# One pool of eight PSUM banks in place of four fixed shares, in a two-layer transformer block on one core

## The chip, the core and the metric

The kernel runs on one core of a Trainium2 chip. The metric is the device time of one execution in microseconds (us). The program is written with a tile framework: the code names tiles, pools and operations, and a scheduler orders each engine's instructions when the program is built. The chip then runs five fixed streams, one for each engine, that wait for each other by semaphores.

## What is computed

Two layers of a diffusion-transformer block work on 256 tokens x and 256 context tokens ctx of width 1024. Each layer projects both, runs three branches (a neighbourhood attention, a gated MLP and a multi-head latent attention with rank-compressed keys), merges them under sigmoid gates, and applies a squared-ReLU MLP:

```python
h = modulate(rms_norm(x, g_norm1[i]), sh1, sc1)
p = h @ w_in[i]
y_na = merge_heads(neighbourhood_attention(q_na, k_na, v_na, k_na_c, v_na_c, na_rpb[i]))
y_gm = spatial_gating(gelu(u), gelu(v), gm_ln_g[i], gm_ln_b[i], gm_w_s[i], gm_b_s[i])
y_mla = merge_heads(dense_attention(q_mla, concat(k_mla_c, k_mla), concat(v_mla_c, v_mla)))
mix = (g0 * (y_na @ na_w_o) + g1 * (y_gm @ gm_w_o) + g2 * (y_mla @ mla_w_o)) @ w_out
x_new = x + gt1 * mix
x_new = x_new + gt2 * squared_relu_mlp(modulate(rms_norm(x_new, g_norm2[i]), sh2, sc2), w1, w2)
```

In layer 0 the context tokens take the same way, as a second stream that attends to itself alone. In layer 1 they only give keys and values.

## The kernel before

Activations lie transposed (features on partitions, 512 tokens on the free axis: 256 of x, 256 of ctx). Large products run as three fp32r matmuls (`mm3`, lines 287 to 289): weights are split in a high and a low part by ScalarE (`wh`, line 115) and VectorE (`wl`, line 116). Each weight block of 512 KB is loaded by SyncE into one of three `raw` buffers.

A layer runs through these stages: projections (`gemm_b`, tiles `b_ps`), the `u` blocks of the gated MLP, neighbourhood attention (NA), the merge of the gated-MLP branch (`merge`: eight pairs of a `gate` and a `z` block), key, value and query products of the latent attention (MLA; tiles `kv`, `qm`, transposes `h_tr`), MLA attention, the merges of the two other branches, the output product and norm, then the MLP (`f1_chunk`, tiles named `f`, and `out_chunk`, tiles `o_ps`).

Both attentions go through `soft_pv`, once for each of four pairs of heads. For each stream v and each half qt of its queries it runs one step for the pair: two score tiles `S` on TensorE (line 410 and 411 in NA, 417 in MLA); then for each head a bias add on VectorE (line 443, NA and stream x only), the row maximum `nm` (445), the exponential with its row sum on ScalarE (448), the reciprocal (450) and the scaling of `P` on VectorE (451), the transposes of `P` into a tile `pt` on TensorE (454) and the copy of `pt` to `PT` on ScalarE (456). After two steps the products with the values go to a tile `pv` or `pvm` (460). Rows are 512 keys wide for x and 256 for ctx. `P` and `PT` have two buffers each.

`soft_pv` notes each score matmul in `marks`, and the following merge takes them as its pace: `gemm_a` ties each three matmuls of a gate or z block behind one mark on TensorE (`issue_after`), so that they may stand between the score matmuls of the attention and not ahead of them.

Every PSUM tile is one bank (128 x 512 fp32) and comes from `psum(tag, name)` at lines 47 and 48. The tag is `mm` for gemm tiles, `s` for score tiles, small transposes and sums, `pt` for the transposes of `P` and two modulation sums, `pv` for attention outputs and the broadcast norm. Tiles of one tag share its banks: 4, 2, 1 and 1. The scheduler takes instructions by priority, which is the order of the code (a block under `high_priority` counts as 400 places earlier), as soon as their inputs and their tiles' buffers are there.

The norm at the end of a stage (`norm_stream`, lines 237 to 247) adds squares over chunks (`sumsq`: ScalarE line 255, VectorE line 256), sums over partitions on TensorE (`st_ps`), takes a power on GpSimd (line 241), builds a diagonal on VectorE (244) and broadcasts it on TensorE (`rstd_b`, line 247).

Of the kernel before, what the change touches and what calls it, by code (L numbers as in the profile page):

```python
# [7 lines left out]
F32 = mybir.dt.float32  # L8
# [18 lines left out]
def hybrid_block_kernel(tc, a, out):  # L27
# [3 lines left out]
    mm = nc.tensor.matmul  # L31

    from contextlib import ExitStack, nullcontext
    with ExitStack() as es:
        def pool(name, bufs=1, **kw):
            return es.enter_context(tc.tile_pool(name=name, bufs=bufs, **kw))
# [8 lines left out]
        pp = pool("ps", space=PSUM)  # L45

        def psum(tag, name):
            return pp.tile([128, 512], F32, tag=tag, name=name, bufs={"mm": 4, "s": 2, "pt": 1, "pv": 1}[tag])


        def g2(name, dt=F32R):
# [88 lines left out]
        def mod_finish(ps, w, dsts, modT, bmod, streams):  # L140

            t = tmp2("mod_sb")
            vec.tensor_copy(t[:, :w], ps[:, :w])
            pst = psum("s", "mod_t")
            for i in range(w // 128):
                nc.tensor.transpose(pst[:, i * 128:(i + 1) * 128], t[:, i * 128:(i + 1) * 128], ident)
            for i in range(w // 128):
                v4 = pst[:, i * 128:(i + 1) * 128].rearrange("p (j r) -> p j r", j=4)
                for v in range(streams):
                    o, b = dsts(modT[:, v, :], i), dsts(bmod, i)  # L150
                    i0 = v4[:, :, v]
                    if len(o.shape) == 3:
                        i0 = i0.rearrange("p (a b) -> p a b", a=2)
                    vec.tensor_tensor(out=o, in0=i0, in1=b, op=ALU.add)

        def mod_quarter(l, q, modT, bmod, streams):

            ps = psum("pt", "mod_ps")
            for kb in range(4):
                for kk in range(2):  # L160
                    raw = g2("rawm", F32)
                    nc.sync.dma_start(out=raw, in_=a["wmod1"][l, q, kb][:, kk * 512:kk * 512 + 512])
                    mod_cols(ps, raw, 0, 128, 2 * kb + kk)
                yield
            mod_finish(ps, 128, lambda m, i: m[:, 0:16].rearrange("p (a c) -> p a c", a=2)[:, :, 2 * q:2 * q + 2], modT,
                       bmod, streams)

        def mod_group(l, g, modT, bmod, streams):
            ps = psum("mm", "mod_ps")
            for k in range(KC):  # L170
                raw = load(a["wmod"][l, g - 2, k])
                mod_cols(ps, raw, 0, 256, k)
                yield
            mod_finish(ps, 256, lambda m, i: m[:, 8 * g:8 * g + 8].rearrange("p (j i) -> p j i", i=2)[:, :, i], modT, bmod,
                       streams)
# [371 lines left out]
        for l in range(L):  # L547
# [192 lines left out]
            for j in range(4):  # L740
# [6 lines left out]
                pv = psum("pv", "pv")  # L747
# [94 lines left out]
            for j in range(4):  # L842
                pv = psum("pv", "pvm")
# [226 lines left out]
```

## Time and profile before

| | |
|---|---|
| median of three runs | 1402.77 us (1400.9 to 1403.62) |
| profiled execution, its own time | 1402.83 us |
| its span in the trace | 1400.8 us |
| TensorE busy | 1370.2 us, 98% |
| VectorE busy | 957.4 us, 68% |
| ScalarE busy | 704.7 us, 50% |
| mean granted TensorE clock | 1.00 |

The page gives one profiled execution. Its busy times are unions over an engine's instructions; TensorE's matmuls overlap each other, so the mean duration of one is longer than its distance to the next.

### The profile page before, as it was taken

What the parts mean: (1) busy time and instruction counts of PE and PEld (TensorE: products, weight loads), DVE (VectorE), ACT (ScalarE), POOL (GpSimd) and SP (SyncE); (2) the same over time, 40 slices, a digit from 0 to 9 for tenths busy, and PEclk for the clock granted to TensorE, in tenths of its full rate; (3) what the DMA queues carried; (4) which work ended last, traced back from release to release, by engine and by line L of the source; (5) the groups of instructions that cost most, each with busy time, mean ns of one, the idle gap of its engine ahead of it and who ended that gap; (6) DMA issues with size and microseconds to landing.
All of it is one profiled execution on the core that took longest, in us unless ns stands there. A gap on an engine that the chain in (4) does not pass through costs nothing.

```text
span 1400.8 us, 22572 instructions
## 1 busy us (share of the span) xinstructions
PE 1370.2 (98%) x8438; PEld 1161.8 (83%) x8438; DVE 957.4 (68%) x2071; ACT 704.7 (50%) x1440; POOL 56.9 (4%) x35
## 2 busy tenths in 40 slices
PE   6999999999999999999999999999999999999999
PEld 4788767777676789988888888988888878999998
DVE  4666477665563558899766665786787766877775
ACT  3466256443453346623324233566676665656654
POOL 0110000110000000000000000011002100000000
PEclk9999999999999999999999999999999999999999
DMA  9423542234313465665555552443543434566664
GB/s 331 142 84 106 187 150 90 71 105 123 119 46 114 127 195 168 208 202 172 203 205 188 175 197 89 150 137 94 181 136 99 136 91 136 181 181 180 183 183 148
DMA packets 67214, 210.61 MB, mean 150 GB/s; under 512 B 8609, under 2 KB 9633, under 8 KB 67105
## 3 DMA queue, kind: packets, MB, share of 16 engines
q1 hardware_dynamic: 67104, 209.18, 46.6%
q8 instruction: 66, 1.08, 0.3%
q14 instruction: 44, 0.35, 0.1%
HBM read 208.10 MB, written 1.05 MB: 149 GB/s over the span
## 4 chain that ended last, share of the span: by engine, by line
PE 96%; DVE 1%; DMA 1%; ACT 1%; issue 0%; SPq 0%; POOL 0%; ACTq 0%; DVEq 0%
PE o_ps L287 8%; PE o_ps L289 8%; PE o_ps L288 8%; PE f L288 6%; PE f L287 6%; PE f L289 6%; PE gate L287 5%; PE gate L288 5%; PE gate L289 5%; PE b_ps L287 5%; PE b_ps L288 4%; PE b_ps L289 4%; PE pt L454 3%; PE S L417 2%; PE z L287 2%; PE z L289 2%
## 5 line engine op out<-in xcount | busy, mean ns | idle before, releaser
L115 ACT ACTIVATE wh<-raw 128x512 fp32r<-128x512 f32 (+1 forms) x570 | 353.1, 626 | 515.8 <-PE o_ps L288 179.7
L116 DVE TENSOR_TENSOR wl<-raw,wh 128x512 fp32r<-128x512 f32 (+1 forms) x570 | 385.8, 683 | 178.1 <-ACT wh L115 172.7
L289 PE MATMUL f<-hH,wl 128*128 128x258 f32 (+2 forms) x560 | 180.9, 324 | 0.1
L287 PE MATMUL f<-hH,wh 128*128 128x258 f32 (+2 forms) x560 | 180.4, 323 | 0.5 <-ACT wh L115 0.5
L288 PE MATMUL f<-hL,wh 128*128 128x258 f32 (+2 forms) x560 | 180.4, 324 | 0.2 <-DVE hL L277 0.2
L288 PE MATMUL o_ps<-aL,wh 128*128 128x256 f32 (+1 forms) x544 | 176.1, 327 | 0.0
L287 PE MATMUL o_ps<-aH,wh 128*128 128x256 f32 (+1 forms) x544 | 176.0, 328 | 0.0
L289 PE MATMUL o_ps<-aH,wl 128*128 128x256 f32 (+1 forms) x544 | 175.6, 328 | 0.0
L287 PE MATMUL gate<-hH,wh 128*128 128x512 f32 (+1 forms) x384 | 140.5, 366 | 0.0
L289 PE MATMUL gate<-hH,wl 128*128 128x512 f32 (+1 forms) x384 | 130.3, 339 | 0.0
L288 PE MATMUL gate<-hL,wh 128*128 128x512 f32 (+1 forms) x384 | 130.1, 339 | 0.0
L287 PEld LDWEIGHTS f<-hH,wh 128*128 128x128 f32 x560 | 106.0, 190 | 9.1 <-ACT wh L115 0.7
L289 PEld LDWEIGHTS f<-hH,wl 128*128 128x128 f32 x560 | 106.2, 190 | 8.5 <-DVE wl L116 0.3
L288 PEld LDWEIGHTS f<-hL,wh 128*128 128x128 f32 x560 | 105.9, 190 | 8.5 <-DVE hL L277 0.4
L287 PEld LDWEIGHTS o_ps<-aH,wh 128*128 128x128 f32 x544 | 102.7, 190 | 9.5 <-ACT aH L937 0.8
L288 PEld LDWEIGHTS o_ps<-aL,wh 128*128 128x128 f32 x544 | 103.1, 190 | 8.5
L289 PEld LDWEIGHTS o_ps<-aH,wl 128*128 128x128 f32 x544 | 102.7, 190 | 8.8
L288 PE MATMUL b_ps<-wl,hH 128*128 128x512 f32 (+2 forms) x288 | 108.8, 381 | 0.0
L289 PE MATMUL b_ps<-wh,hL 128*128 128x512 f32 (+2 forms) x288 | 106.3, 381 | 0.0
L287 PE MATMUL b_ps<-wh,hH 128*128 128x512 f32 (+2 forms) x288 | 103.7, 385 | 0.0
L200 DVE SCALAR_TENSOR_TENSOR macc<-rawx,sS,macc 128x512 f32<-128x512 f32 x112 | 78.9, 748 | 32.7 <-DMA rawx<-in_wmod_dram 32.4
L287 PEld LDWEIGHTS gate<-hH,wh 128*128 128x128 f32 x384 | 72.7, 189 | 15.9 <-issue 7.5
(229 smaller groups left out, 2481.3 us busy)
## 6 DMA issues: line engine op xcount, KB each, us to landing
raw<-in_wa_dram SPq DMA_DIRECT2D x147, 512.0 KB, 3.6
raw<-in_w_dram SPq DMA_DIRECT2D x68, 512.0 KB, 3.6
raw<-in_wb_dram SPq DMA_DIRECT2D x32, 512.0 KB, 3.3
raw<-in_wmod_dram SPq DMA_DIRECT2D x32, 512.0 KB, 3.4
rawx<-in_wmod_dram SPq DMA_DIRECT2D x32, 512.0 KB, 4.5
raw<-in_wo_dram SPq DMA_DIRECT2D x24, 512.0 KB, 3.6
rawm<-in_wmod_dram SPq DMA_DIRECT2D x32, 256.0 KB, 6.0
rawx<-in_wmod_dram SPq DMA_DIRECT2D x32, 256.0 KB, 4.2
```

What stands on the lines that cost most here:

```text
L115: act(out=wh[:, :width], in_=src, func=AF.Copy)
L116: vec.tensor_tensor(out=wl[:, :width], in0=src, in1=wh[:, :width], op=ALU.subtract)
L200: summed = vec.scalar_tensor_tensor(out=o, in0=src, scalar=s, in1=o, op0=ALU.mult, op1=ALU.add)
L287: mm(ps, lhsT=sh, rhs=mh, start=first, stop=False)
L288: mm(ps, lhsT=sh, rhs=ml, start=False, stop=False)
L289: mm(ps, lhsT=sl, rhs=mh, start=False, stop=last)
L417: return mm(s, lhsT=Q[h][0:96, q0:q0 + 128], rhs=K[h][0:96, k0:k0 + nk], start=True, stop=True)
L454: nc.tensor.transpose(pt[:, i * 128:(i + 1) * 128], P[:, i * 128:(i + 1) * 128], ident)
```

## The change

```diff
         def psum(tag, name):
-            return pp.tile([128, 512], F32, tag=tag, name=name, bufs={"mm": 4, "s": 2, "pt": 1, "pv": 1}[tag])
+            return pp.tile([128, 512], F32, tag="bank", name=name, bufs=8)
```

All PSUM tiles now carry one tag with eight buffers. The argument `tag` is no longer used. The arithmetic and the number of banks are the same. The scheduler makes another order of it, on all engines.

TensorE in neighbourhood attention of layer 0, x stream, before. `S`, `pt` and `pv` are the attention's tiles, `z` and `yg` belong to the merge of the gated-MLP branch:

```order
L460 MATMUL pv<-PT,vna 64x256 x4
L454 MATMUL pt<-ident,P 128x128 x4
L410 MATMUL S<-naK,naQ 128x512
L411 MATMUL S<-naK,naQL_1070 128x512
L287 MATMUL z<-yg,wh 128x512
L288 MATMUL z<-yg,wh 128x512
L289 MATMUL z<-yg,wl 128x512
L454 MATMUL pt<-ident,P 128x128 x4
L410 MATMUL S<-naK,naQ 128x256
L411 MATMUL S<-naK,naQL_1064 128x256
```

The same place now:

```order
L410 MATMUL S<-naK,naQ 128x512
L411 MATMUL S<-naK,naQL_1064 128x512
L410 MATMUL S<-naK,naQ 128x512
L411 MATMUL S<-naK,naQL_1070 128x512
L460 MATMUL pv<-PT,vna 64x256 x4
L454 MATMUL pt<-ident,P 128x128 x8
L410 MATMUL S<-naK,naQ 128x512
L411 MATMUL S<-naK,naQL_1064 128x512
L410 MATMUL S<-naK,naQ 128x512
L411 MATMUL S<-naK,naQL_1070 128x512
L454 MATMUL pt<-ident,P 128x128 x8
L460 MATMUL pv<-PT,vna 64x256 x8
```

Before, a single score tile, three merge matmuls and four transposes take turns. Now both score tiles of a step stand together, then both heads' transposes; the merge's matmuls have moved behind the last step of the attention. Both attentions of both layers read like this.

TensorE at the norm after the output product of layer 0, before (the x half of the chunks ends some 35 matmuls ahead of `st_ps`):

```order
L289 MATMUL o_ps<-mix,wl 128x256
L287 MATMUL o_ps<-mix,wh 128x256
L288 MATMUL o_ps<-mix,wh 128x256
L237 MATMUL st_ps<-ones,acc_4950 128x1 x2
L289 MATMUL o_ps<-mix,wl 128x256
L287 MATMUL o_ps<-mix,wh 128x256
L288 MATMUL o_ps<-mix,wh 128x256
```

Here `rstd_b` comes another 34 matmuls behind `st_ps`.

The same place now:

```order
L288 MATMUL o_ps<-mix,wh 128x256
L289 MATMUL o_ps<-mix,wl 128x256
L237 MATMUL st_ps<-ones,acc_4950 128x1 x2
L247 MATMUL rstd_b<-diag,ones 128x256
L287 MATMUL o_ps<-mix,wh 128x256
L288 MATMUL o_ps<-mix,wh 128x256
```

Before, 34 matmuls of the ctx half stood between `st_ps` and `rstd_b`, and 35 ahead of `st_ps`. Now `st_ps` follows the last matmul of the x half and `rstd_b` follows `st_ps`. The norms at the end of layer 0 and after the output product of layer 1 have moved in the same way; the two norms of the ctx half in layer 0 still have matmuls ahead of `rstd_b`, but none ahead of `st_ps`.

## Rows read from the trace of the kernel before

**Rows 1.** The page: span, busy time of engines, chain that ended last.

```profile
span 1400.8 us, 22572 instructions
...
PE 1370.2 (98%) x8438; PEld 1161.8 (83%) x8438; DVE 957.4 (68%) x2071; ACT 704.7 (50%) x1440; POOL 56.9 (4%) x35
...
PE 96%; DVE 1%; DMA 1%; ACT 1%; issue 0%; SPq 0%; POOL 0%; ACTq 0%; DVEq 0%
```

**Rows 2.** Stretches (NA, MLA, NA, MLA, MLP): length, busy PE, PEld, DVE, ACT, POOL; clock; DMA.

```profile
183.00:252.00 69.00, 66.82 (x403) 46.97 (x404) 50.43 (x132) 43.57 (x112) 0.00 (x0) 1.00 0.33 107
331.00:435.00 104.00, 104.00 (x551) 72.35 (x550) 58.23 (x138) 50.80 (x125) 0.00 (x0) 1.00 0.30 92
1010.00:1063.00 53.00, 48.52 (x355) 41.32 (x355) 40.06 (x96) 35.08 (x77) 0.00 (x0) 1.00 0.43 127
1107.00:1163.00 56.00, 53.09 (x355) 40.29 (x354) 32.93 (x73) 32.91 (x74) 0.00 (x0) 1.00 0.25 76
1190.00:1225.00 35.00, 35.00 (x292) 34.95 (x292) 28.12 (x62) 22.07 (x45) 0.70 (x1) 1.00 0.61 185
```

**Rows 3.** Timeline, end of MLA in layer 1: start, us, engine, line, [idle before].

```profile
1152.00 1.95 PE L460 MATMUL pvm<-PT,vml 128*64 128x256 f32 x16
...
1157.85 0.68 ACT L448 ACTIVATE P<-S,nm 128x512 f32<-128x512 f32 x1
...
1158.65 0.16 DVE L450 RECIPROCAL r<-sm 128x1 f32<-128x1 f32 x1 [0.91 <-ACT P L448]
...
1158.92 0.49 DVE L451 TENSOR_SCALAR P<-P,r 128x512 f32<-128x512 f32 x1
...
1159.56 0.63 PE L454 MATMUL pt<-ident,P 128*128 128x128 f32 x4 [0.89 <-DVE P L451]
1160.22 0.60 ACT L456 ACTIVATE PT<-pt 128x512 f32<-128x512 f32 x1 [0.93 <-PE pt L454]
...
1160.87 1.95 PE L460 MATMUL pvm<-PT,vml 128*64 128x256 f32 x16 [0.69 <-ACT PT L456]
```

**Rows 4.** Groups by form, VectorE: count, busy us, mean ns, idle before.

```profile
L869 DVE SCALAR_TENSOR_TENSOR xT<-o_ps,modT,xT 128x256 f32<-128x256 f32 x120 | 54.6, 480 | 38.8 <-PE o_ps L289 38.2
L445 DVE TENSOR_REDUCE nm<-S 128x1 f32<-128x512 f32 x64 | 43.8, 686 | 19.4 <-PE S L417 18.8
L256 DVE TENSOR_TENSOR acc<-acc,sq 128x256 f32<-128x256 f32 x49 | 20.2, 420 | 6.1 <-ACT sq L255 5.6
L443 DVE TENSOR_TENSOR S<-S,bias 128x256 f32<-128x256 f32 x32 | 13.6, 428 | 2.7 <-PE S L411 2.6
L445 DVE TENSOR_REDUCE nm<-S 128x1 f32<-128x256 f32 x32 | 13.5, 423 | 20.8 <-PE S L417 13.5 <-PE S L411 7.3
L451 DVE TENSOR_SCALAR P<-P,r 128x256 f32<-128x256 f32 x32 | 11.2, 351 | 0.8
```

**Rows 5.** Groups by form, ScalarE.

```profile
L255 ACT ACTIVATE sq<-xT 128x256 f32<-128x256 f32 x49 | 20.1, 414 | 6.0 <-DMA xT<-in_xT_dram 3.7 <-DVE xT L869 1.0 <-DVE acc L256 0.2
L448 ACT ACTIVATE P<-S,nm 128x256 f32<-128x256 f32 x32 | 15.0, 470 | 0.0
```

**Rows 6.** Chain of waits: start, length, instruction; NA and MLA of layer 1.

```profile
1015.87 0.50 PE S L410
...
1018.04 0.23 PE S L410
1018.27 0.23 PE S L411
...
1111.03 0.86 PE S L417 x2
```

**Rows 7.** Timeline of TensorE at the first norm.

```profile
12.50 1.01 PE L237 MATMUL st_ps<-ones,acc 128*128 128x1 f32 x4
...
15.84 1.22 PE L247 MATMUL rstd_b<-diag,ones 128*128 128x256 f32 x2
```

**Rows 8.** DMA issues: tile, queue, count, KB each, us to landing.

```profile
bias<-in_nab_dram SPq DMA_DIRECT2D x16, 256.0 KB, 3.2
```

## The prediction

> **What bounds the kernel now.** I read the page first: TensorE is busy for 1370.2 of 1400.8 us, and the chain that ended last is TensorE for 96% [rows 1]. Only some 30 us of the span are TensorE's idle time, so nothing that makes another engine faster can bring more than that, while any order that leaves TensorE without work costs its full length. Next I read the busy time of the four attention stretches [rows 2]. There the softmax runs on VectorE and ScalarE, a chain of dependent instructions, and yet TensorE is busy for 66.8 of 69, 104 of 104, 48.5 of 53 and 53.1 of 56 us: its idle time in all four is 2.2 + 0 + 4.5 + 2.9 = 9.6 us. The reader is to see that the merge's gate and z matmuls fill the waits of the softmax. The third view is the end of the MLA attention of layer 1 [rows 3], one place where the fill has run out before the attention has. There TensorE waits 0.89 us for `P` and 0.69 us for `PT`, in the middle of the softmax of one last head.
>
> **The change: what the two tables of the order say.** It adds and removes no instruction, no byte and no bank. What it changes is which tile may be taken first. With one tag, tiles seem to be handed out in the order of the code: a gate tile is asked for after all attention tiles, and the score tiles of the next step after the `pt` tiles of this one. So the order has lost both its covers: no merge matmul between the steps, and no score matmul of the next step ahead of the transposes of this one. TensorE takes its stream in order, so from the last score of a step to the last transposes it waits for both softmaxes. I cost this step by step.
>
> *One step of MLA, 512 keys.* Two score tiles at 0.86 us [rows 6]: 1.7 us, 1.8 with the first one's start from idle. The second head's row maximum takes 0.69 us [rows 4], up to 2.5. From the start of its exponential to its first transpose the trace shows 1159.56 - 1157.85 = 1.71 us (exponential and row sum, reciprocal, scaling and the hops between) [rows 3], up to 4.2. Four transposes take 0.63 us [rows 3]: some 4.9 us a step. TensorE has 2 x 0.86 + 2 x 0.6 = 2.9 us of work in it, so it idles 2.0 us.
>
> *One step of NA, 512 keys.* The first score tile is done after 0.50 + 0.23 us; a matmul of 512 columns in the stream takes 0.23 us [rows 6]. Then VectorE has bias, maximum, bias, maximum: 2 x (0.43 + 0.69) = 2.24 us [rows 4], up to 3.0. Then 1.71 and 0.63 us as above: 5.4 us. TensorE's work is 4 x 0.23 + 1.2 = 2.1 us, idle 3.3 us.
>
> *The ctx steps, 256 keys.* The maximum is 0.42 us, and the exponential and the scaling shorten the 1.71 us by 0.21 and 0.13 us to 1.37 us [rows 3 to 5]; scores and transposes are halved. ScalarE takes the two exponentials one behind the other, 0.56 us each with the row sum. MLA comes to 3.3 us with 1.5 us of work, idle 1.8; NA to 3.2 with 1.1, idle 2.1.
>
> *How many.* Four pairs, two halves: 8 steps a stretch and stream. 512 keys: 16 in NA, 16 in MLA (two layers). 256 keys: 8 and 8 (layer 0 alone). Idle: 16 x 3.3 + 16 x 2.0 + 8 x 2.1 + 8 x 1.8 = 53 + 32 + 17 + 14 = 116 us.
>
> *The products with the values.* After each second step of stream x TensorE waits for the last `PT` copy, 0.69 us [rows 3], 16 times: 11 us. The ctx products (half of 1.95 us [rows 3]) stand behind the next pair's scores and fill 6 x 0.95 = 6 us of idle already counted. Net 5 us. The copies of `pv` on both engines fall into the next chain in 12 places, for at most 12 x 0.69 = 8 us and at least nothing, and the first step of each stretch starts behind other work on these engines: I take 8 us for both, between 0 and 12. Attention in sum: 116 + 5 + 8 = 129 us, in place of the 9.6 us there now: **+119 us**.
>
> *The norms.* In three places `st_ps` now stands right behind the last matmul of its sum and `rstd_b` right behind `st_ps`. Ahead of `st_ps`: 0.48 + 0.41 + 0.42 = 1.3 us (residual add, square, sum) [rows 4, 5]. Between the two, at the first norm: 15.84 - 13.51 = 2.3 us, with other work in VectorE's way [rows 7]; without that 1.5 us at the least, so 1.9. Three times 3.2 us, and twice 1.3 us where only the first wait is bare: **+12 us**, bounds 8 and 15. The pooled modulation sums are now followed at once by their transposes, which wait for a 512-column pass on VectorE (the nearest row is 0.69 us [rows 4]), twice: +2 us, bounds 1 and 4. The start of the program and the transposes around the MLA products are also bunched; no row prices them, bounds 0 (they hide behind loads) and 10, I take 4, near the row of one norm wait.
>
> *What stays covered.* The gate and z matmuls that follow the attention in a block have their own weights to split: that is what the MLP stretch does now, with TensorE at 35.00 of 35 us and 185 GB/s [rows 2], so I cost them at nothing. If that cover were gone, each block would wait for a weight load. Of the queues, SyncE's has moved: six bias loads stand together ahead of the merge's next weights, and each pair waits for the buffer of the pair before. A bias lands 3.2 us after its issue [rows 8], while between its buffer's release in the second step of a pair and its use lie some 4 us of that step and 2.6 us of value products, so nothing. GpSimd has only the norms' powers; nothing there moves past another.
>
> Sum: 119 + 12 + 2 + 4 = 137 us on the profiled execution's own 1402.83 us (its span plus 2 us), which is the median's 1402.77 within 0.1 us: **1540 us**, 10% slower. About 0.2% is what a measurement here tells from no change.
>
> **The rivals.**
>
> *Faster: eight banks take away the bank waits there are.* In its favour: TensorE's idle of 30 us, of which 9.6 lie in the attention; with the 12 us before the first load taken off and 2 at the end, 16 us could go: 1387 us. For this a step's chain, 4.9 or 5.4 us, must be shorter than what stands between scores and transposes on TensorE; in the new order nothing stands there. Chance 0.02. The Trainium skill, "Perfetto Trace Analysis", section "Matmul Optimizations", asks that all eight PSUM banks be used for the most parallelism between instructions, which would speak for this case. The four shares already add up to eight banks, and the rows on the stretches show TensorE fed by them, so I give the rule no more than that chance.
>
> *Slower, but less: the heads overlap until VectorE is the bound.* If a step's scores reached ahead of the transposes before, VectorE alone would set the step: NA 2 x (0.43 + 0.69 + 0.16 + 0.49) = 3.5 us against 2.1 of TensorE, MLA 2.7 against 2.9. Idle 16 x 1.4 + 16 x 0.4 (ctx steps) = 29 us and the 11 for `PT`, less 9.6, plus 18 elsewhere: +48 us, 1451 us. Against it: `S` stands behind `pt` on TensorE in every step shown. Chance 0.06.
>
> *Much slower: the clock.* The granted clock is 1.00 (2.4 GHz) in every stretch [rows 2]. In the new attention TensorE would be at work for some 137 of 266 us in four stretches. If the clock fell to 1.2 GHz there, scores and transposes would double on the path: about +1.3 us a step of NA, +2.1 of MLA, +0.7 and +1.0 for ctx, 16 x 3.4 + 8 x 1.7 = 68 us, and 16 x 1.95 = 31 for the products: 1640 us. Against it: the end of MLA in layer 1 has the same gaps, and the 16 product records there take 1.95 us as in the filled stretch ahead of it [rows 3]. Chance 0.14. The Trainium skill, "TensorE: Matmul & The Clock Gate", section "What's actually happening", says that the default is the throttled state and that activity releases it; by that the long sparse stretches could lose it, and the clock's row in the new profile decides.
>
> *The tags are only names:* the same eight banks give the same time. The order speaks against it. Chance 0.01.
>
> **How the numbers follow.** Forecast 0.77 at 1540 us; its own bounds come from 20% either way on the chains (23 us) and the bounds above: 1500 to 1580. The range reaches to both sides for the neighbours: 1490 to 1620, where the upper part takes in a clock that falls for some of the time. Left out: the lesser rival, both small ones, half of the clock case, about 0.17. Faster 0.02, same 0.01, slower 0.97.
>
> **What would show it.** Right: the four stretches last about 80, 78, 54 and 50 us without a gate matmul in them and TensorE is idle near half of each; waits of `pt` for `P` in the chain, some 80 of them; about 3 us of idle at three norms; MLP stretches unchanged. Wrong: merge matmuls inside the attention, idle below 60 us there, a clock below 1.00, or new waits for weights in the merges.

## The result, and the profile after

The changed kernel takes **1609.12 us** (median of 4 runs, 1606.83 to 1610.1) beside 1403.19 us for the kernel before (4 runs, 1400.9 to 1406.09): a ratio of 1.146 with a 95% interval of 1.144 to 1.149. It is slower by 206 us. The forecast was 1540 us with a range of 1490 to 1620.

The page of the changed kernel, the lines that answer to [rows 1]:

```profile
span 1604.8 us, 22605 instructions
...
PE 1454.0 (91%) x8438; PEld 1205.3 (75%) x8438; DVE 971.2 (61%) x2071; ACT 717.5 (45%) x1440; POOL 56.8 (4%) x35
...
PE 77%; issue 11%; DVE 6%; ACT 3%; DMA 2%; SPq 0%; POOL 0%; POOLq 0%; ACTq 0%; DVEq 0%
```

Two numbers say nearly all. TensorE's idle time, span less busy time, went from 30.6 us to 1604.8 - 1454.0 = 150.8 us: **+120 us**. And TensorE's busy time went from 1370.2 to 1454.0 us, **+84 us**, for the same 8438 matmuls. The mean granted clock, 1.000 before, is 0.937. The chain that ended last is TensorE for 77% of the span; the 11% of "issue" in it are nearly all one step of 160.5 us, for which the profile shows no release, so little is to be read from that share.

The windows of the four attention stretches, from the first score to the end of the last product with values (NA and MLA of layer 0, NA and MLA of layer 1), and one MLP stretch; columns as in [rows 2]:

```profile
180.30:281.70 101.40, 64.44 (x284) 40.18 (x284) 49.71 (x136) 41.49 (x106) 0.00 (x0) 0.71 0.07 21
370.50:460.80 90.30, 65.03 (x285) 34.47 (x284) 39.82 (x109) 39.76 (x104) 0.00 (x0) 0.87 0.02 6
1125.50:1191.30 65.80, 40.59 (x164) 25.14 (x162) 31.80 (x82) 25.77 (x56) 0.00 (x0) 0.68 0.09 25
1256.80:1325.10 68.30, 50.38 (x162) 24.71 (x161) 21.96 (x51) 24.89 (x56) 0.00 (x0) 0.67 0.00 1
```

```profile
1440.00:1475.00 35.00, 35.00 (x294) 35.00 (x293) 24.66 (x50) 18.53 (x34) 0.00 (x0) 1.00 0.60 185
```

The four stretches last 101.4 + 90.3 + 65.8 + 68.3 = 325.8 us where the forecast had 80 + 78 + 54 + 50 = 262. TensorE is idle for 105 us of them (length less busy time), and the granted clock, the third column from the right, is 0.67 to 0.87 in place of 1.00 [rows 2]. The MLP stretch is as it was: all busy, clock 1.00, 185 GB/s.

TensorE's waits, in columns of total us, times and longest. The two of `pt` that lead in the kernel before:

```profile
PE pt L454 <- ACT PT L456: 2.9, 4, 0.7
PE pt L454 <- DVE P L451: 1.8, 2, 0.9
```

And in the changed kernel:

```profile
PE pt L454 <- DVE P L451: 50.9, 41, 7.7
PE pt L454 <- DVE r L450: 35.2, 20, 2.8
...
PE pv L460 <- ACT PT L456: 5.5, 8, 0.7
PE pvm L460 <- ACT PT L456: 5.5, 8, 0.7
```

The transposes wait for the softmax (`P` and the reciprocal `r`) for 86 us, and each of the 16 groups of products with the values of stream x waits 0.69 us for the last copy.

TensorE's timeline shows what the clock does to a step. A step of MLA with 512 keys in layer 0 at a clock of 1.00 (start, length, instruction, idle before):

```profile
419.34 1.88 PE L417 MATMUL S<-kml,qml 96*128 96x512 f32 x4
422.77 0.63 PE L454 MATMUL pt<-ident,P 128*128 128x128 f32 x4 [1.55 <-DVE P L451]
423.63 0.63 PE L454 MATMUL pt<-ident,P 128*128 128x128 f32 x4 [0.23 <-DVE P L451]
424.95 1.95 PE L460 MATMUL pvm<-PT,vml 128*64 128x256 f32 x16 [0.69 <-ACT PT L456]
```

The same scores one step ahead of it, and products and scores in NA of layer 0:

```profile
240.27 3.68 PE L460 MATMUL pv<-PT,vna 128*64 128x256 f32 x16 [0.69 <-ACT PT L456]
...
251.14 0.63 PE L410 MATMUL S<-naK,naQ 128*128 128x512 f32 x1
251.57 0.63 PE L411 MATMUL S<-naK,naQL 128*128 128x512 f32 x1
...
412.62 3.62 PE L417 MATMUL S<-kml,qml 96*128 96x512 f32 x4
```

The four score records take 3.62 us in place of 1.88, the sixteen products 3.68 in place of 1.95, and two score matmuls of 512 columns in the stream stand 0.43 us apart in place of 0.23 [rows 6].

### The profile page after: what moved, and what is told of

Same layout as the page of the kernel before. It is cut to its first block, busy times and chain, and to the rows that moved or that the text cites. A ratio compares the mean times of both kernels' runs of the same rounds, so it can differ in the third digit from the quotient of the medians.

```text
span 1604.8 us, 22605 instructions
## 1 busy us (share of the span) xinstructions
PE 1454.0 (91%) x8438; PEld 1205.3 (75%) x8438; DVE 971.2 (61%) x2071; ACT 717.5 (45%) x1440; POOL 56.8 (4%) x35
## 4 chain that ended last, share of the span: by engine, by line
PE 77%; issue 11%; DVE 6%; ACT 3%; DMA 2%; SPq 0%; POOL 0%; POOLq 0%; ACTq 0%; DVEq 0%
PE o_ps L288 7%; PE o_ps L287 7%; PE o_ps L289 7%; PE f L288 6%; PE f L287 6%; PE f L289 6%; PE b_ps L287 4%; PE b_ps L289 4%; PE b_ps L288 4%; PE gate L287 4%; PE gate L288 3%; PE gate L289 3%; PE pt L454 3%; PE pv L460 2%; DVE nm L445 2%
## 5 line engine op out<-in xcount | busy, mean ns | idle before, releaser
L454 PE MATMUL pt<-ident,P 128*128 128x128 f32 x320 | 67.2, 349 | 94.4 <-DVE P L451 50.9
L454 PEld LDWEIGHTS pt<-ident,P 128*128 128x128 f32 x320 | 43.4, 173 | 131.0 <-issue 93.4
L287 PE MATMUL gate<-hH,wh 128*128 128x512 f32 (+1 forms) x384 | 133.9, 349 | 0.0
L445 DVE TENSOR_REDUCE nm<-S 128x1 f32<-128x512 f32 (+1 forms) x96 | 56.5, 599 | 82.3 <-PE S L417 54.8
```

The costliest lines, as they stand in the source:

```text
L287: mm(ps, lhsT=sh, rhs=mh, start=first, stop=False)
L445: vec.tensor_reduce(out=nm, in_=s[:, :nk], axis=AX.X, op=ALU.max, negate=True)
L454: nc.tensor.transpose(pt[:, i * 128:(i + 1) * 128], P[:, i * 128:(i + 1) * 128], ident)
```

## The experiments

Theory: with one tag the banks are handed out in the order of the code. That costs two things at once. The gate and z tiles, which the code asks for after the last attention tile, and the next step's scores, asked for after this step's `pt`, no longer cover the softmax (the idle time); and the TensorE that is left sparse loses its clock (the busy time). The rivals: sharing banks costs by itself; the norms carry more than was thought; the added busy time isn't the clock.

All runs in one table. Clock, idle and busy time are those of one profiled execution of each kernel (with code order it was the longest of five, 1491.1 us). "Real busy" is TensorE's busy time; for the two kernels with useless products it is the time that the records of all other matmuls cover. Each ratio is to runs of the kernel before on the same chip (medians of 1401.2 to 1403.4 us):

| kernel | median us | ratio to before (95%) | clock | TensorE idle us | real busy us |
|---|---|---|---|---|---|
| before | 1403.2 | | 1.000 | 30.6 | 1370.2 |
| changed | 1609.1 | 1.146 (1.144 to 1.149) | 0.937 | 150.8 | 1454.0 |
| mm apart | 1440.2 | 1.027 (1.025 to 1.028) | 0.996 | 60.2 | 1377.3 |
| norms apart | 1595.5 | 1.136 (1.133 to 1.139) | 0.941 | 136.9 | 1450.5 |
| s with mm | 1483.7 | 1.057 (1.055 to 1.059) | 0.978 | 73.4 | 1408.1 |
| useless products, 416 | 1558.7 | 1.110 (1.108 to 1.112) | 0.988 | 74.1 | 1388.5 |
| useless products, 272 | 1558.3 | 1.112 (1.110 to 1.114) | 0.985 | 94.5 | 1399.1 |
| code order | 1481.7 | 1.057 (1.055 to 1.059) | 0.975 | 94.2 | 1394.8 |
| code order, norms apart | 1469.1 | 1.049 (1.046 to 1.051) | 0.978 | 78.4 | 1390.3 |
| scores ahead too | 1448.1 | 1.032 (1.031 to 1.034) | 0.989 | 67.5 | 1378.8 |
| the same, four shares | 1430.6 | 1.021 (1.018 to 1.024) | 0.995 | 43.3 | 1382.5 |
| pt with pv | 1408.1 | 1.004 (1.003 to 1.005) | 0.996 | 34.1 | 1373.8 |
| s with pt | 1428.1 | 1.018 (1.017 to 1.019) | 0.998 | 53.0 | 1373.8 |

### Which tiles must not share

*mm apart.*

```diff
-            return pp.tile([128, 512], F32, tag="bank", name=name, bufs=8)
+            return pp.tile([128, 512], F32, tag="mm" if tag == "mm" else "att", name=name, bufs=4)
```

> The banks in two groups: four for the tag mm (gate, z, o_ps and the other matrix products), four shared by all other tags (S, pt, pv, and the norms' st_ps and rstd_b). The theory: with one tag a bank is handed out in the order of the code, so the gate and z tiles of the merge, which the code asks for after the last attention tile, cannot start beside the attention; TensorE stands about 120 us more, and in the sparse stretches its clock falls, which costs the other 84 us of the 206. With mm apart both come back: 1403 to 1425 us, mean granted clock 0.99 to 1.00, TensorE idle 30 to 50 us. Rival A, sharing banks among attention tiles is itself what costs (S, pt and pv still share one group here): over 1500 us, clock below 0.96. Rival B, the norms carry a large part: they are spread again here too, so this run does not tell it apart from the theory; the next one does.

Measured: 1440.2 us, clock 0.996. The page:

```profile
PE 1377.3 (96%) x8438; PEld 1165.2 (81%) x8438; DVE 959.7 (67%) x2071; ACT 706.1 (49%) x1440; POOL 57.0 (4%) x35
```

Of the 204 us in the profiled executions 167 are back, 91 us of idle time and 77 us of busy time, with the clock. So most of the loss lies in gate and z sharing with the attention, and the clock comes back with the cover. The time is 15 us above what I expected: some 37 us stay, though gate and z are free.

*s with pt* and *pt with pv* look for these 37 us. Both start from the four shares of before; the first gives s and pt three banks together, the second pt and pv two.

```diff
+            return pp.tile([128, 512], F32, tag="spt" if tag in ("s", "pt") else tag, name=name, bufs={"mm": 4, "pv": 1}.get(tag, 3))
```

```diff
+            return pp.tile([128, 512], F32, tag="turn" if tag in ("pt", "pv") else tag, name=name, bufs=4 if tag == "mm" else 2)
```

> Four banks for mm and one for pv as before the change; s and pt share three. In code order a step asks for S, S, pt, pt, so the next step's second S takes the bank of this step's first pt, and can't be made before that transpose's copy has ended; before the change the scores ran a step ahead. The theory: part of the 37 us that s, pt and pv in one group of four lost comes from here: 1405 to 1435 us, TensorE idle 32 to 55 us. If the 37 us come from pv in the group alone: 1398 to 1406 us.

> Four banks for mm and two for s as before the change; only pt and pv share, two banks in place of one each. The order of requests: pv of a pair of heads, then its pt, then the next pv, so a pt can only be late where the next pair's pv has taken the second bank. The theory (a shared group costs where its tiles are asked for early and used late): hardly anything is, so 1398 to 1410 us, clock 1.00. Rival A, sharing among the attention tiles costs by itself, as the 37 us that the run with s, pt and pv in one group of four lost against the kernel before could mean: 1415 to 1440 us.

Measured: 1428.1 and 1408.1 us, 26 and 6 us above the 1402.2 us of the kernel before in the same runs. TensorE's waits with s and pt in one group:

```profile
PE pt L454 <- DVE P L451: 19.9, 27, 2.0
```

In this kernel's trace the transposes of both heads stand ahead of the next step's scores. So most of the 37 us are scores that no longer run ahead of the transposes, as the theory has it; 6 us come from pt sharing with pv. The two make 32; whether the rest comes from all three sharing at once was not tried. None of these divisions beats the four shares: the best is 0.4% slower.

*s with mm.* Six banks for gate, z and the scores, one for pt, one for pv.

```diff
+            return pp.tile([128, 512], F32, tag="bank" if tag in ("mm", "s") else tag, name=name, bufs=6 if tag in ("mm", "s") else 1)
```

> Six banks shared by mm and s, one for pt, one for pv. Scores may now run up to six tiles ahead of the transposes (which wait for one bank of their own), but gate and z stand behind all scores of the four heads pairs. The theory: the cover of the attention stays lost, and since the scores run ahead a step is no longer scores, softmax, transposes in a row but the work of VectorE and ScalarE in a row: the stretches shrink towards the bound by VectorE (1451 us was worked out for it) but TensorE stays sparse and its clock low: 1470 to 1570 us, mean clock 0.92 to 0.98. Rival A, sharing among the attention tiles is what costs: it is gone here, so 1403 to 1430 us. Rival D, one group with the scores costs as much as one group with all: 1595 to 1625 us.

Measured: 1483.7 us, clock 0.978. Here the scores run ahead, and in all four stretches the first gate matmul stands behind the last score; from there on gate and z do fill between the transposes that are left. NA of layer 1 up to its first gate matmul and as a whole, the instructions of gate tiles alone (length, PE, PEld, ACT; clock; DMA):

```profile
1069.00:1100.30 31.30, 0.00 (x0) 0.00 (x0) 0.00 (x0) 0.78 0.20 60
1069.00:1129.00 60.00, 16.76 (x123) 15.38 (x123) 1.87 (x5) 0.89 0.31 95
```

Idle time is 43 us more than before the change, busy time 38 us more. The prediction's lesser rival, heads that overlap until VectorE is the bound, had +48 us of idle time. That is near the 43, but it reckoned without the fill behind the last score, so the run doesn't test that sum.

### The norms

```diff
+            return pp.tile([128, 512], F32, tag=name if name in ("st_ps", "rstd_b") else "bank", name=name, bufs=1 if name in ("st_ps", "rstd_b") else 6)
```

> One pool of six for all but the norms; st_ps and rstd_b get a bank each of their own, so that the norms' small products stand among other products again (34 and 35 matmuls from st_ps to rstd_b, as before the change). The theory: the norms were priced at 12 us (8 to 15), so 1594 to 1601 us, clock in the attention as low as with eight banks. Rival B, the norms carry more than a tenth of the loss: below 1588 us. Rival C, it is the number of banks in the one pool that matters (six here): over 1620 us.

Measured: 1595.5 us (four runs, 1589.4 to 1599.0), 13.6 us less than the changed kernel. The timeline of TensorE in the changed kernel shows three norms bare at both places, and as the second here (654.37) one of the two in which only `st_ps` is:

```profile
632.89 0.58 PE L237 MATMUL st_ps<-ones,acc 128*128 128x1 f32 x4 [1.81 <-DVE acc L256]
635.10 1.19 PE L247 MATMUL rstd_b<-diag,ones 128*128 128x256 f32 x2 [1.64 <-DVE diag L244]
...
654.37 0.61 PE L237 MATMUL st_ps<-ones,acc 128*128 128x1 f32 x4 [1.72 <-DVE acc L256]
...
1009.58 0.58 PE L237 MATMUL st_ps<-ones,acc 128*128 128x1 f32 x4 [1.82 <-DVE acc L256]
1011.79 0.67 PE L247 MATMUL rstd_b<-diag,ones 128*128 128x256 f32 x2 [1.63 <-DVE diag L244]
...
1411.31 0.61 PE L237 MATMUL st_ps<-ones,acc 128*128 128x1 f32 x4 [1.72 <-DVE acc L256]
1413.46 1.22 PE L247 MATMUL rstd_b<-diag,ones 128*128 128x256 f32 x2 [1.54 <-DVE diag L244]
```

Their waits in sum, in the changed kernel:

```profile
PE st_ps L237 <- DVE acc L256: 8.8, 5, 1.8
PE rstd_b L247 <- DVE diag L244: 6.9, 4, 2.1
```

Of these 15.7 us, 2.05 stand at the first norm of the program, which the forecast priced with the start; the waits at the five other norms that stand bare make 13.6 us. Six banks in the pool in place of eight made nothing worse, so the number of banks isn't the point, and the norms carry some 14 of the 206 us.

### The clock

If the added 84 us are the clock, then work that nobody needs, put where TensorE idles, must make the kernel faster.

```diff
+            return pp.tile([128, 512], F32, tag="idle" if tag == "idle" else "bank", name=name, bufs=1 if tag == "idle" else 7)
...
                         S.append(s)
+                    with tc.issue_after(marks[-1]):
+                        for _ in range(10 if v == 0 else 6):
+                            mm(idle, lhsT=hH[0][:, 0:128], rhs=hH[1], start=True, stop=True)
```

> One pool of seven, and the eighth bank takes useless products (512 columns, nothing reads them): 10 behind the scores of each step of the x half, 6 behind those of the context half, in both attentions of both layers: 384 of them, some 85 us of TensorE at the full clock, put where it idles 1.8 to 3.3 us a step. Everything else is as in the changed kernel. The theory: the idle time stays what it is (the useless products fill part of it), but the clock holds, so the real products of the stretches take their full-clock times: 1609 less up to 84, plus what does not fit into the idle time: 1520 to 1560 us, granted clock 0.98 to 1.00 in the stretches. Rival E, the 84 us of added busy time are not the clock but the products waiting on banks or on their operands: the useless products come on top, 1609 to 1690 us.

Measured: **1558.7 us, 50 us faster with 416 matmuls more** (there are 32 steps of x and 16 of ctx, so 416 and not the 384 that the expectation counted). The page, and TensorE's groups by form of the useless products, the transposes and the products with values (count, busy us, mean ns, idle before):

```profile
span 1557.3 us, 23418 instructions
...
PE 1483.2 (95%) x8854; PEld 1250.9 (80%) x8854; DVE 972.3 (62%) x2071; ACT 715.0 (46%) x1440; POOL 57.1 (4%) x35
```

```profile
L443 PE MATMUL idle<-hH 128*128 128x512 f32 x416 | 114.0, 419 | 0.0
L458 PE MATMUL pt<-ident,P 128*128 128x128 f32 x320 | 51.0, 287 | 15.3 <-DVE P L455 6.8 <-ACT yg L736 3.7 <-DVE r L454 3.5
...
L464 PE MATMUL pv<-PT,vna 128*64 128x256 f32 x160 | 19.9, 387 | 5.6 <-ACT PT L460 5.6
L464 PE MATMUL pvm<-PT,vml 128*64 128x256 f32 x160 | 19.9, 387 | 5.9 <-ACT PT L460 5.9
```

The same groups of the changed kernel without them:

```profile
L454 PE MATMUL pt<-ident,P 128*128 128x128 f32 x320 | 67.2, 349 | 94.4 <-DVE P L451 50.9 <-DVE r L450 35.2 <-ACT yg L732 4.8
...
L460 PE MATMUL pv<-PT,vna 128*64 128x256 f32 x160 | 35.4, 614 | 5.5 <-ACT PT L456 5.5
L460 PE MATMUL pvm<-PT,vml 128*64 128x256 f32 x160 | 30.7, 546 | 5.5 <-ACT PT L456 5.5
```

The records of useless and real matmuls overlap, so 1483.2 - 114.0 is not the real ones' time. Counted from the trace with the useless records left out, the real matmuls cover 1388.5 us, 65.5 less than the 1454.0 of the changed kernel, on banks that are still handed out from one pool; the products with the values are back from 35.4 and 30.7 to 19.9 us. So work that nobody needs gives back 65.5 of the 84 us, and 28.9 us of real work are still at the low clock in this run.

That nearly all of the 84 us are the clock follows from the trace of the changed kernel itself. Its mean clock of 0.937, over two levels, makes 201 us at 1.2 GHz, and by its records 168.8 us of TensorE's busy time lie in them. At the ratios of the rows above (3.62 to 1.88 and 3.68 to 1.95 us) this work would take some 80 us less at the full clock, an estimate; where the last few us come from was not followed up.

The useless products cover 1483.2 - 1388.5 = 94.7 us by themselves. They filled 150.8 - 74.1 = 76.7 us of idle time, and the other 18.0 came on top: 1604.8 - 65.5 + 18.0 = 1557.3 us. The granted clock of the four stretches is 0.96, 1.00, 0.94 and 0.96:

```profile
178.40:266.00 87.60, 76.31 (x412) 54.07 (x412) 49.00 (x136) 40.97 (x106) 0.00 (x0) 0.96 0.08 25
354.80:439.60 84.80, 81.55 (x413) 54.66 (x412) 39.62 (x108) 38.90 (x103) 0.00 (x0) 1.00 0.02 7
1104.80:1161.10 56.30, 47.01 (x245) 33.90 (x244) 31.94 (x82) 26.29 (x59) 0.00 (x0) 0.94 0.11 34
1226.50:1279.50 53.00, 50.04 (x245) 33.24 (x244) 22.60 (x51) 24.11 (x57) 0.00 (x0) 0.96 0.00 1
```

*Fewer of them:* 7 and 3 in place of 10 and 6.

> The run with useless products again (one pool of seven, the eighth bank for them), with 7 in place of 10 behind the scores of an x step and 3 in place of 6 in a context step: 272 in all in place of 416. They took 274 ns each and 37 us of their 114 came on top of the idle time they filled. The theory: at 75 us they fit into the 77 us that the 416 had filled; if the clock holds with fewer too, the time is 1604.8 less 85 us, 1515 to 1535 us. If it doesn't hold, the real products slow again and the time stays at 1540 to 1600 us.

Measured: 1558.3 us, the same as with 416. That lies in the second range, but not for its reason: the real matmuls didn't fall back. The clock held nearly (0.985), and they cover 1399.1 us, 10.6 more than with 416. The useless products cover 1461.7 - 1399.1 = 62.6 us by themselves, 32.1 fewer, and TensorE stands idle for 94.5 us, 20.4 more (its idle time ahead of the transposes is 36.9 us in place of 15.3). The three cancel. My reckoning, that 37 us had come on top and could be saved, rested on busy times that overlap: by the records 18.0 us came on top with 416 and 62.6 - (150.8 - 94.5) = 6.3 with 272, so there was little to gain.

### The order of the code

If banks go out in the order of the code, then rewriting the code should bring the cover back from one pool.

```diff
                         S.append(s)
+                    for _ in range(nfill[v]):
+                        next(fill, None)
...
+            fill = merge_parts(l, 0, ygH, ygL, hH, hL, ymix, T, range(0, n0))
...
-            merge(l, 0, ygH, ygL, hH, hL, ymix, T, range(0, n0), paced(marks, 12 * n0 - FREE, FREE))
+            for _ in fill:
+                pass
```

Here `merge_parts` is the loop of `merge` as a generator that pauses after each 12 matmuls.

> One pool of eight, as in the changed kernel, but the code is written in another order: the merge's gate and z products are cut into pieces of 12 matmuls, and the attention asks for a piece (one to three, as the stretch needs) between the two scores of a step and their transposes. The theory, that banks are handed out in the order of the code and that this is why the cover went: the cover is back, at 2.8 us a piece against idle times of 1.8 to 3.3 us a step; what stays is the norms' and the start's some 14 us (as the run with their banks apart showed) and what the pieces don't fill: 1415 to 1470 us, granted clock 0.98 to 1.00, TensorE idle 45 to 95 us. Rival F, one pool as such costs (the pool, its size or the sharing, whatever the order): over 1540 us, clock below 0.96.

> The run before, with the two banks of the norms (st_ps, rstd_b) taken out of the pool, six left for the rest. The theory: the two parts add up, so 10 to 16 us less than the run before: 1400 to 1458 us. If the norms' share depended on the attention's order, it would be under 5 us less; if six banks were too few for this order, more time than the run before.

> The run before it with the norms apart (one pool of six, pieces of the merge in the attention's code), with two more changes of code order: a step's scores are asked for before the transposes of the step ahead of it, across the pairs of heads too, as they ran before the change, and the merge's pieces are half as long (6 matmuls). That run is still 67 us over the kernel before. The theory: 25 to 37 us of these are scores that no longer run a step ahead (what s and pt in one group cost with mm apart), the rest pieces that end too early; so 1410 to 1445 us, clock 0.98 to 1.00, TensorE idle 35 to 60 us. If sharing costs by itself, whatever the order: 1460 us or more.

Measured: 1481.7, 1469.1 and 1448.1 us. The order of the code alone, with the pool of eight untouched, takes back 127 of the 206 us, so the pool as such is not the cause of the bulk. Taking the norms out gives 12.6 us, nearly the 13.6 that they gave in the other order. The third run gives 21 us more; it asks for the scores a step ahead, writes both softmaxes ahead of both heads' transposes and halves the pieces, and which of these brings the 21 us it can't tell. The three runs lie 12, 11 and 3 us over the ranges that I gave: each step went in the direction expected and left more than expected.

*The same code with the four shares* asks who owns the 45 us left.

```diff
+            return pp.tile([128, 512], F32, tag=tag, name=name, bufs={"mm": 4, "s": 2, "pt": 1, "pv": 1}[tag])
```

> The code of the run before it (scores a step ahead, pieces of the merge inside the attention), but with the four shares of before the change, 4, 2, 1 and 1, in place of the pool. It tells where the 45 us come from that that run still loses to the kernel before. If they belong to the pool (a shared bank costs even in this order): 1400 to 1415 us. If they belong to the code as rewritten (which piece stands where, the background sums that the pieces call), and the pool costs nothing more once the code is in order: 1435 to 1455 us. In between, both.

Measured: 1430.6 us, in between. So some 29 us (ratio 1.021) belong to my rewriting of the code, and some 17 us (the loss of 45 us less these 29) still to the pool. For these 17 us there are rows but no run: one of TensorE's largest waits with the pool is that of the background sums' transposes,

```profile
PE mod_t L146 <- DVE mod_sb L143: 8.2, 3, 6.9
```

which with the four shares is 0.4 us. Whether the rest of the 17 us would go with another order stays open.

## Why the prediction was right, and which term it lacked

**The order and the two lost covers: right.** No gate or z matmul stands in the four stretches ahead of their last transposes (14 and 15 gate matmuls stand between these and the last products of the two stretches in layer 0); mm apart brings most of it back, and code order brings most of it back from the pool itself. Both covers that the prediction names are real, the second, scores ahead of transposes, worth 26 us when it alone is taken away, by s and pt in one group. Of the some 80 waits of `pt` that were to show, 61 did, 41 for `P` and 20 for `r`.

**The price of a step: right at the full clock, for MLA.** MLA with 512 keys was put at 4.9 us; the rows from 419.34 to 424.26 us give 4.92. The 16 waits for the last `PT` copy were put at 11 us; the trace has 5.5 + 5.5. NA was not read in this way: its clock changes within the steps. For all four stretches the run with 416 useless products comes nearest to the sum's premise of a full clock: 87.6 + 84.8 + 56.3 + 53.0 = 281.7 us, some 18 of them useless work on top, beside the forecast's 262.

**The idle time: 17 us too high.** The sum had 137 us more, the trace has 120. TensorE idles for a third of the stretches, not near half. In the stretches it is 105 us against 129; elsewhere 24 us more than before against the 18 of norms, pooled sums and start. A part of the difference may be the clock itself (slower scores and transposes of one head run while the other head's softmax does, and so fill idle time), which was not tried alone.

**The norms: right.** +12 us with bounds of 8 and 15; 13.6 us by the run, and 13.6 us of waits at the five norms it names (the run has the program's first norm in it too, so the agreement to the tenth is chance). The three fully bare ones stand idle for 1.81 + 1.64, 1.82 + 1.63 and 1.72 + 1.54 us against the 3.2 forecast. The pooled sums were 4.4 us against 2, a little above their bound of 4.

**The clock: the step that failed.** The sum took every matmul at its full-clock duration, on the argument that the gaps at the end of MLA in layer 1 had left the products at 1.95 us [rows 3], and put the fall at a chance of 0.14 beside it. It is a term of the sum: TensorE's busy time grew by 84 us, some 80 of them by the clock. "A clock below 1.00" was one of the forecast's own signs of being wrong, and it came. The rows it rested on show one gap of 0.89 us and one of 0.69 us behind 50 us of filled work; they say nothing of 66 to 101 us made of such gaps, many of them 1.4 to 2.8 us long, and that was the difference to see. The rival, on its part, priced a clock of 1.2 GHz all through at 100 us and 1640 us in all; the stretches have 0.67 to 0.87. The truth is the forecast's mechanism with most of the rival's price: 1609 us, 69 over the point and 29 over the sum's own bounds of 1500 to 1580. That it lies in the range at all it owes to the part that was added for a clock "that falls for some of the time", and in part to luck: the idle time was 17 us too high and took that much off the miss.

**What was to stay, stayed.** The MLP stretch is unchanged, no wait of a gate or z matmul for weights stands among TensorE's waits, and a bias load lands in 3.0 us against 3.2 [rows 8]:

```profile
bias<-in_nab_dram SPq DMA_DIRECT2D x16, 256.0 KB, 3.0
```

**Eight banks for more parallelism: not here.** The rule of the Trainium skill, "Perfetto Trace Analysis", section "Matmul Optimizations", is met by both kernels, and by all the others of this study: each uses eight banks. What set the time was which tile could ask for one first.

## What to carry to other kernels

A share of banks for one kind of tile is also a right to run ahead: a pool common to all kinds hands its banks out in the order of the code, and whatever is written later and was meant to fill gaps can't start. Before merging pools, ask of each tile which fill was written behind it. And where a change makes TensorE's stream sparse, price its clock as a term of the sum: here it was some 80 of 204 us, and work without use, put in the gaps, brought 50 us back.

## What was not expected of the hardware

The clock falls in the middle of work, not only in a pause, and comes and goes within one stretch. Windows of 4 us in NA of layer 0 of the changed kernel (length, TensorE busy, granted clock, DMA share, GB/s):

```profile
204.00:208.00 4.00, 2.64 (x10) 0.50 0.00 0
208.00:212.00 4.00, 3.48 (x16) 0.68 0.00 0
212.00:216.00 4.00, 1.36 (x8) 1.00 0.36 113
...
256.00:260.00 4.00, 3.64 (x12) 0.50 0.00 0
260.00:264.00 4.00, 1.93 (x8) 0.50 0.00 0
```

It has two levels, 1.00 (2.4 GHz) and 0.50 (1.2 GHz); values between are windows that hold both. At 256 us TensorE was at work for 3.64 of 4 us at the low level, behind gaps of 2 us, and at 212 us it had the full level in a window in which it worked for 1.36 us: so the level of a window isn't set by the work in that same window. The Trainium skill, "TensorE: Matmul & The Clock Gate", section "Wait — 56ns, not 53.3ns?", has matmuls in a row start 426.7 ns apart at 512 columns when the array is cold; the scores at 251.14 and 251.57 us agree with 0.43 us.
